# Weight blocks begun one block ahead, and more projection pairs in seven products, in a two-layer encoder trunk

## Chip, cores and metric

The kernel runs on one core of a Trainium2 chip. The metric is the device time of one execution in microseconds (us); three runs of the kernel before took 2011.72, 2015.77 and 2019.56 us, median 2015.77.

## What is computed

Two layers of an encoder over 256 positions of width 2048. Layer 0 mixes positions by dilated window attention, layer 1 by a spatial gate; both run a cross-attention into 256 memory tokens beside the mixer, and both end in a gated FFN with a width-3 convolution. The weight products take nearly all of the time:

```python
for i in range(DEPTH):                       # DEPTH = 2
    h = rmsnorm(x, mix_norm_g[i])
    mem_n = rmsnorm(mem, mem_norm_g[i])
    proj = einsum('bsd,df->bsf', h, a_w_in[j] or b_w_in[j])
    tok = mixer_a(proj[..., :3 * A_QKV_W])   # layer 1: mixer_b(proj[..., :2 * B_W], ...)
    mem_out = memory_cross_attention(proj[..., -MEM_W:], mem_n, w_mem_kv[i])
    x = x + einsum('bsf,fd->bsd', concatenate([tok, mem_out]), w_out)
    h = rmsnorm(x, ffn_norm_g[i])
    x = x + conv_ffn(h, ffn_w_up[i], ffn_conv_w[i], ffn_conv_b[i], ffn_w_down[i])
return rmsnorm(x, final_norm_g)
```

## The kernel before, in words

All weights stream from HBM once, in blocks of 128 x 2048 float32 (1 MB). Products are made at nearly float32 precision from float16 parts: a block is split into `whi` (the rounded value) and `wlo` (the rest), the activations likewise, and a product is hi x hi + hi x lo + lo x hi.

`project_t` (L156 ff.) makes one **pair**: two output tiles of 128 columns for 256 positions, from one or more blocks of up to eight 128-row slices. A pair over the full width of 2048 has two blocks. A block comes in two forms, made by `block_t`:

- *Unformed*: ACT makes `whi` (L138), DVE `wlo` (L139), and TensorE (PE) runs 48 matmuls of 256 columns, 12,288 columns in all.
- *Formed*: the 2 x 2 product of half blocks is made with seven products instead of eight. ACT makes `whi` (L144) and rescales `raw` (L145), DVE makes two halves of `wlo` (L146, L147) and the sums `ws2` and `ws41` (L148, L149; both shown as `ws`), and PE runs 72 matmuls of 256 or 128 columns, 11,264 columns in all. The activations' sums come from `form_sums` (L215 ff.). At the pair's end the parts are put together: ACT copies one part to `wr` (L207), DVE adds (L208, L209, L211, L212), and only then the pair's consumer runs. The last product of a block, into `acc`, reads `ws41`.

In the FFN (`ffn`, L463 ff.) 44 up pairs alternate between gate and value half. Behind each pair ACT runs six taps of the convolution (L481, L482, L483 twice), DVE adds them (L484, L485); behind a gate pair ACT runs the GELU (L487), behind a value pair DVE multiplies (L489) and ACT and DVE split the result into `act` (L246, L247). `UP_FORM` sets which up pairs are formed: the second and fourth of every five, 18 of 44 per FFN. Then eight down pairs follow, seven of them formed in 32 of 44 slices. In the first mixer's input projection every second pair of the loop is formed, in the second mixer's projections none.

A layer's stages follow each other in the program: norm, mixer projections, attention or gate, output projection, norm, up, down. `norm_ready` (L348 ff.) is the norm before an FFN: DVE multiplies (L357) and splits (L247). While it runs, PE works on the memory keys for layer 1 (`kvk`, second pair). In `mixer_b` the value projection `binv` is followed on ACT by two squares (L632), a root with its table load (L261) and the splits of the normalized values (L250), before the pairs of `bin` go on.

The order of the work: a scheduler orders each engine's instructions at build time, by the place in the program and by which buffers are free. There are three `wlo` and `whi` buffers (four `whi` in the FFN), three `raw` buffers (five in the FFN), two of each `ws`, three `acc` and two `accb` banks. Small steps that need not run at once (attention heads, sums) wait in a list, and `step()` runs one of them at the head of each block and in its middle. `fine` counts blocks that are split in four pieces. `keep_clock` runs matmuls without use while PE would idle in a norm.

Of the kernel before, what the change touches and what calls it, by code (L numbers as in the profile page):

```python
# [9 lines left out]
F16 = mybir.dt.float16  # L10
F32 = mybir.dt.float32
# [5 lines left out]
P = 128  # L17
T = 256
# [29 lines left out]

UP_FORM = (False, True, False, True, False)
IN_FORM = (False, True)  # L50
DOWN_K = 32
WARM = (36, 32, 36, 24)


# [5 lines left out]
def trunk(ctx: ExitStack, tc: tile.TileContext, xT, memT, par, w, wsT, sbias, out):  # L60
# [35 lines left out]

    def next_of(name, dtype):
        r = more.get(name, rings[name])
        turns[name] = (turns[name] + 1) % len(r)
        return r[turns[name]].tile([P, KC * FG], dtype, name=name)  # L100

    def block_n(name, g, c, loads=1, beside=None):
        step()
        pieces = FINE if fine[0] > 0 else PIECES
# [16 lines left out]
    def block_t(name, g, k0, kc, form):  # L121

        step()
        pieces = max(1, FINE * kc // KB) if fine[0] > 0 else PIECES
        fine[0] -= 1
        raw = next_of("raw", F32)
        hi = next_of("whi", F16)
        lo = wsp.tile([P, KC * FG], F16, name="wlo")
# [27 lines left out]
    def project_t(name, g, act, nk, evac, sums=None, form=0, before=None, kb=KB):  # L156
        a = acc.tile([P, FG], F32, name="acc")
        b = accb.tile([P, FG], F32, name="accb") if form else None
        done = [0, 0]
        blocks = [(k0, min(kb, nk - k0)) for k0 in range(0, nk, kb)]  # L160
        last = [blocks[-1][0] + blocks[-1][1], min(form, nk)]
# [63 lines left out]
    def project_n(name, g, act, nk, evac, before=None, loads=1, beside=None):  # L225
        ps = [acc.tile([P, FG], F32, name="acc") for _ in range(2)]
        for c in range(nk // KC):
            if before is not None:
                before(c)
            hi, lo = block_n(name, g, c, *((loads, beside) if c == 0 else ()))  # L230
# [208 lines left out]

    def residual(name, act, nk, scale, squares, halves=False, last=False, sums=None, form=0, gain=None):  # L440
        def add_out(g, src):
# [16 lines left out]
        for g in range(KD // 2):  # L458
            project_t(name, g, act, nk, add_out, sums, form if g > 0 else 0)

    xact, xsum = lambda k: xs[:, k, :], lambda k: xu[:, k, :]

    def ffn(i, squares):  # L463
        with tc.tile_pool(name=f"ffw{i}", bufs=1) as fw, tc.tile_pool(name=f"ffr{i}", bufs=2) as fwr, \
# [5 lines left out]
            for g in range(FT):  # L470
# [26 lines left out]
            residual(f"down{i}", lambda k: act[:, k, :], FT, 1.0 / (SW * S_ACT), squares, last=i == 1,  # L497
                     sums=lambda k: room(k, 1)[:, 0, :], form=DOWN_K)
            more.clear()
# [3 lines left out]
    def mixer_a(later):  # L503
        with tc.tile_pool(name="ma", bufs=1) as mp, tc.tile_pool(name="mat", bufs=2) as mt:
# [25 lines left out]

            pending.extend(mem_attention(cat, 0, S_CAT[0]) + [masks] + later)
            sums_later()
            for g in range(3):
                project_n("ainv", g, xs, KD, v_out(g))
# [52 lines left out]
            for g in range(2 * NH * NG // 2):  # L587
                project_t("ain", 2 + g, xact, KD, qk_out, xsum, KD if IN_FORM[g % 2] else 0)
                while done < NH and (done + 1) * 2 * NG <= (g + 1) * 2:
# [11 lines left out]
    def mixer_b():  # L601
        with tc.tile_pool(name="mb", bufs=1) as mp:
            cat = mp.tile([P, BG + NH, 2 * T], F16, name="cat")
            v = mp.tile([P, 2, BG * P], F32, name="v")
            vs = xu.rearrange("p k c -> p (k c)")[:, :4 * BG * P].rearrange("p (t i c) -> p t i c", t=2, i=2)
# [21 lines left out]
            with tc.tile_pool(name="mbt", bufs=2) as mt:  # L627
# [62 lines left out]
    with tc.tile_pool(name="own0", bufs=1) as op:  # L690
        own_tiles(op)
        with tc.tile_pool(name="sums", bufs=1) as sums:
# [27 lines left out]
            for g in range(2):  # L720
                project_t("kv0k", g, mact, KD, k_out, before=lambda c, g=g: x_in(2 * g + c))
            nc.sync.dma_start(out=prm[:, C_CW:], in_=par[:, C_CW:])
            for g in range(2):
                project_t("ain", g, xact, KD, qm_out)
# [102 lines left out]
```

## Time and profile before

| | |
|---|---|
| median of 3 runs | 2015.77 us |
| profiled execution | 2014.48 us |
| its span in the trace | 2012.7 us |
| mean granted clock of TensorE | 0.995 |
| PE busy | 1968.0 us, 98% of the span |
| DVE busy | 1609.1 us, 80% |
| ACT busy | 1418.5 us, 70% |

The span runs from the first to the last instruction of the profiled execution; 1.8 us of its time lie outside. The trace shows for every instruction its start, its length, the idle time of the engine ahead of it and what ended that idle time. The granted clock is the share of 2.4 GHz that TensorE got; it has two levels, 1.2 and 2.4 GHz.

### The profile page before, as it was taken

Reading aid. Unit: us, or ns where it says so; the run is one execution under the profiler, and the core shown is the slowest. Engines: PE = TensorE matmul, PEld = TensorE weight load, DVE = VectorE, ACT = ScalarE, POOL = GpSimd, SP = SyncE. Lnnn points to the kernel's source line nnn. Section 1 sums busy time; section 2 is a strip of 40 time slices with the busy share of each in tenths; the row PEclk is TensorE's granted clock in tenths of the full one; section 3 lists DMA queues with packets and bytes.
Section 4 is the critical chain, followed back from the end, with each engine's and each line's share of the span. In section 5 each row is a group of like instructions: output and inputs, shape, how many; then the busy total and the mean of one; then the engine's idle time right before and its main releaser. Section 6 shows DMA issues by size and latency. Waiting matters only on the chain.

```text
span 2012.7 us, 47883 instructions
## 1 busy us (share of the span) xinstructions
PE 1968.0 (98%) x21200; PEld 1724.7 (86%) x21200; DVE 1609.1 (80%) x1942; ACT 1418.5 (70%) x1649; POOL 2.4 (0%) x9
## 2 busy tenths in 40 slices
PE   8999999999999999999999999999999999999997
PEld 5648888799999999899976489889999999989997
DVE  8867776988888888978877365588888888897885
ACT  7666656887888888666756464577888888866773
POOL 0000000000000000000000000000000000000000
PEclk9999999999999999999999999999999999999999
DMA  8475445656555666466655365546566566645661
GB/s 318 172 259 202 168 151 185 242 206 209 205 210 209 210 210 210 172 216 222 221 210 201 134 212 195 201 179 220 210 210 210 210 210 210 210 168 211 230 221 53
DMA packets 59391, 407.72 MB, mean 203 GB/s; under 512 B 6704, under 2 KB 7344, under 8 KB 12720
## 3 DMA queue, kind: packets, MB, share of 16 engines
q1 hardware_dynamic: 58896, 400.48, 56.2%
q0 software_dynamic: 288, 4.19, 0.5%
q8 instruction: 165, 2.70, 0.5%
q14 instruction: 42, 0.34, 0.0%
HBM read 400.46 MB, written 4.19 MB: 201 GB/s over the span
## 4 chain that ended last, share of the span: by engine, by line
PE 86%; DVE 8%; ACT 3%; DMA 2%; issue 1%; SPq 0%; DVEq 0%; ACTq 0%
PE acc L164 68%; PE accb L164 12%; PE acc L239 2%; PE acc L240 2%; PE acc L238 2%; DVE wlo L139 1%; DVE wlo L118 1%; PE misc L385 1%; ACT whi L138 1%; DMA raw<-w_ainv 1%; DVE xs L247 0%; ACT whi L117 0%; ACT whi L144 0%; DMA raw<-wsT 0%; DVE xu L222 0%
## 5 line engine op out<-in xcount | busy, mean ns | idle before, releaser
L164 PEld LDWEIGHTS <-whi 128*128 128x128 f16 x10880 | 971.2, 98 | 110.5 <-ACT whi L138 6.3
L164 PE MATMUL acc<-xs,whi 128*128 128x256 f16 (+1 forms) x6592 | 797.6, 266 | 9.6 <-ACT whi L138 5.6
L139 DVE SCALAR_TENSOR_TENSOR wlo<-raw,whi 128x2048 f16<-128x2048 f32 (+2 forms) x286 | 465.6, 1644 | 42.9 <-ACT whi L138 40.0
L164 PEld LDWEIGHTS <-wlo 128*128 128x128 f16 x5440 | 443.4, 98 | 50.8 <-DVE wlo L139 10.4
L138 ACT ACTIVATE whi<-raw 128x2048 f16<-128x2048 f32 (+2 forms) x286 | 391.9, 1391 | 131.4 <-PE acc L164 106.4
L144 ACT ACTIVATE whi<-raw 128x2048 f16<-128x2048 f32 x140 | 267.0, 1907 | 117.5 <-PE acc L164 109.5
L164 PE MATMUL acc<-xs,wlo 128*128 128x256 f16 x2176 | 284.0, 273 | 4.8 <-DVE wlo L139 4.8
L164 PE MATMUL acc<-act,whi 128*128 128x256 f16 x2368 | 278.7, 262 | 0.0
L145 ACT ACTIVATE raw<-raw 128x2048 f32<-128x2048 f32 x140 | 267.4, 1910 | 3.0
L146 DVE SCALAR_TENSOR_TENSOR wlo<-whi,raw 128x1024 f16<-128x1024 f16 x140 | 171.1, 1222 | 93.4 <-PE accb L164 48.0
L164 PEld LDWEIGHTS <-ws 128*128 128x128 f16 x3360 | 193.5, 98 | 1.2 <-DVE ws L149 1.0
L149 DVE TENSOR_TENSOR ws<-whi,ws 128x2048 f16<-128x2048 f16 x140 | 170.8, 1220 | 2.7
L147 DVE SCALAR_TENSOR_TENSOR wlo<-whi,raw 128x1024 f16<-128x1024 f16 x140 | 170.6, 1219 | 0.0
L164 PE MATMUL acc<-xu,whi 128*128 128x128 f16 x896 | 154.0, 219 | 0.0
L164 PE MATMUL accb<-xu,ws 128*128 128x128 f16 x1792 | 119.0, 219 | 0.3 <-DVE ws L149 0.2
L484 DVE TENSOR_TENSOR conv<-conv,tap 128x510 f32<-128x510 f32 x88 | 60.6, 689 | 70.6 <-ACT tap L482 69.6
L481 ACT ACTIVATE conv<-wr,prm 128x256 f32<-128x256 f32 x72 | 42.7, 593 | 101.6 <-DVE wr L212 101.6
L118 DVE SCALAR_TENSOR_TENSOR wlo<-raw,whi 128x512 f16<-128x512 f32 (+1 forms) x56 | 75.9, 1373 | 45.5 <-ACT whi L117 38.9
L148 DVE TENSOR_TENSOR ws<-wlo 128x1024 f16<-128x1024 f16 x140 | 96.4, 689 | 2.7
L117 ACT ACTIVATE whi<-raw 128x512 f16<-128x512 f32 (+1 forms) x56 | 63.6, 1170 | 46.4 <-PE acc L164 19.0
L164 PE MATMUL acc<-cat,whi 128*128 128x256 f16 x768 | 91.7, 273 | 0.0
L238 PE MATMUL acc<-whi,xs 128*128 128x512 f16 x192 | 72.8, 379 | 1.6 <-DVE v L251 1.6
(193 smaller groups left out, 1864.7 us busy)
## 6 DMA issues: line engine op xcount, KB each, us to landing
raw<-w_up SPq DMA_DIRECT2D x176, 1024.0 KB, 4.8
raw<-w_down SPq DMA_DIRECT2D x80, 1024.0 KB, 5.0
raw<-w_ain SPq DMA_DIRECT2D x28, 1024.0 KB, 4.8
raw<-w_bin SPq DMA_DIRECT2D x16, 1024.0 KB, 4.9
raw<-w_bout SPq DMA_DIRECT2D x16, 1024.0 KB, 4.8
raw<-w_ainv SPq DMA_DIRECT2D x12, 1024.0 KB, 4.9
raw<-w_binv SPq DMA_DIRECT2D x12, 1024.0 KB, 4.9
raw<-w_aout SPq DMA_DIRECT2D x8, 1024.0 KB, 4.9
```

Of the source, the lines that this page charges most:

```text
L117: S.activation(hi[:, f], raw[:, f], AF.Copy, scale=SW)
L118: V.scalar_tensor_tensor(lo[:, f], raw[:, f], SW, hi[:, f], op0=ALU.mult, op1=ALU.subtract)
L138: S.activation(h, r, AF.Copy, scale=SW)
L139: V.scalar_tensor_tensor(l, r, SW, h, op0=ALU.mult, op1=ALU.subtract)
L144: S.activation(hi[:, :n], raw[:, :n], AF.Copy, scale=SW)
L145: S.activation(raw[:, :n], raw[:, :n], AF.Copy, scale=SW * CX)
L146: V.scalar_tensor_tensor(l[:, 0, :], h[:, 0, :], -CX, r[:, 0, :], op0=ALU.mult, op1=ALU.add)
L147: V.scalar_tensor_tensor(l[:, 1, :], h[:, 1, :], -1.0 - CX, r[:, 1, :], op0=ALU.mult, op1=ALU.add)
L148: V.tensor_tensor(s2[:, :n // 2], l[:, 1, :], l[:, 0, :], op=ALU.subtract)
L149: V.tensor_tensor(s41[:, :n].rearrange("p (j f) -> p j f", j=2), h, s2[:, :n // 2].unsqueeze(1).to_broadcast([P, 2, n // 2]), op=ALU.add)
L164: PE.matmul((a, b)[bank][:, at:at + n], weights, moving, start=done[bank] == 0, stop=stop)
L238: PE.matmul(ps[t], ah, hi[:, k, :], start=(kk == 0), stop=False)
```

## The change

- `AHEAD = 1`: blocks are made by `block()`, which keeps a plan of all blocks in program order. When a block is asked for, the next one in the plan is begun (load and split written into the program) before the asking block's matmuls. Waiting steps run after that.
- `UP_FORM` becomes (False, True): from the fourth up pair on, every second one is formed, 21 of 44 per FFN in place of 18. The first three are unformed.
- Of the eight pairs of the second mixer's output projection `bout`, three (2, 4, 6) are formed; their sums go to a new tile `cu`.
- The second pair of `kvk` becomes an array of its own, `kvl`, with blocks of eight slices in place of four. Empty steps go between the norm's sums. The clock-keeping matmuls read a tile of ones in place of the identity.

```diff
-UP_FORM = (False, True, False, True, False)
+UP_FORM = (False, True)
+AHEAD = 1
...
+    busy = pool.tile([P, P], F16, name="busy")
...
-    def next_of(name, dtype):
-        r = more.get(name, rings[name])
+    def next_of(name, dtype, ffn=False):
+        r = more.get(name, rings[name]) if ffn else rings[name]
...
+    plan, ready = [], {}
+
+    def block(*key):
+        if key in ready:
+            parts = ready.pop(key)
+        else:
+            assert not plan or plan.pop(0) == key
+            parts = (block_t if len(key) == 5 else block_n)(*key)
+        while plan and len(ready) < AHEAD:
+            k = plan.pop(0)
+            ready[k] = (block_t if len(k) == 5 else block_n)(*k)
+        step()
+        return parts
...
-            parts = block_t(name, g, k0, kc, k0 < form)
+            parts = block(name, g, k0, kc, k0 < form)
...
-            PE.matmul(ps[:, :P], ident16, ident16, start=True, stop=True)
+            PE.matmul(ps[:, :P], busy, busy, start=True, stop=True)
...
         for k in range(0, KD, KC):
+            pending.append(lambda: None)
             pending.append(lambda k=k: form_sums(xu[:, k:k + KC, :], xs[:, k:k + KC, :]))
...
-                project_t(f"up{i}", g, xact, KD, conv, xsum, KD if UP_FORM[g % len(UP_FORM)] else 0)
+                project_t(f"up{i}", g, xact, KD, conv, xsum, up_form(g))
...
-                residual("bout", lambda k: cat[:, k, :], BG + NH, 1.0 / (SW * S_CAT[1]), squares, gain=C_FFN + KD)
+                for k in range(0, BG + NH, KC):
+                    pending.append(lambda k=k: form_sums(cu[:, k:k + KC, :], cat[:, k:k + KC, :]))
+                residual("bout", lambda k: cat[:, k, :], BG + NH, 1.0 / (SW * S_CAT[1]), squares, gain=C_FFN + KD,
+                         sums=lambda k: cu[:, k, :], form=bout_form)
...
+    up_form = lambda g: KD if g > 1 and UP_FORM[g % 2] else 0
+    in_form = lambda g: KD if g > 1 and IN_FORM[g % 2] else 0
+    bout_form = lambda g: BG + NH if g in (2, 4, 6) else 0
+    down_form = lambda g: DOWN_K if g > 0 else 0
...
+            planned("up0", range(FT), KD, up_form)
+            planned("down0", range(KD // 2), FT, down_form)
...
-        project_t("kvk", 1, mact, KD, k_out, kb=KC)
+        project_t("kvl", 0, mact, KD, lambda g, src: k_out(1, src))
```

In the changed kernel the lines move: whi and wlo of an unformed block L163, L164; of a formed one L169 to L174 (as L144 to L149); wr L232 to L237 (as L207 to L212); the taps L510 to L512, GELU L516, DVE's additions L513, L514 and product L518, the split of act L274, L275.

ACT in the up projection, from the last tap of one pair to the wr of the next formed pair. In the order before, in every second case, two unformed blocks stand there (and two formed ones in the others):

```order
L483 ACTIVATE tap2_7160<-acc_7161,prm_82 128x256
L138 ACTIVATE whi_7598<-raw_7597 128x2048
L246 ACTIVATE act_4580<-conv0_6969 128x2x256
L138 ACTIVATE whi_7652<-raw_7651 128x2048
L207 ACTIVATE wr_7454<-accb_7285 128x128
L481 ACTIVATE conv0_7281<-wr_7454,prm_82 128x256
```

In the order after, two formed blocks always:

```order
L512 ACTIVATE tap2_7061<-acc_7062,prm_82 128x256
L169 ACTIVATE whi_7430<-raw_7429 128x2048
L170 ACTIVATE raw_7429<-raw_7429 128x2048
L516 ACTIVATE conv0_7059<-conv0_7059 128x512
L169 ACTIVATE whi_7504<-raw_7503 128x2048
L170 ACTIVATE raw_7503<-raw_7503 128x2048
L232 ACTIVATE wr_7353<-accb_7190 128x128
L510 ACTIVATE conv1_7186<-wr_7353,prm_82 128x256
```

The pattern of the steps is now the same in every two pairs; from the first wr of an FFN to the twentieth it repeats 19 times on ACT, and DVE's steps repeat as often.

DVE ahead of the first FFN's norm, from the sum for it to the norm's first product. Before, the `wlo` here are those of the second `kvk` pair, whose third and fourth blocks are 4501 and 4533:

```order
L446 SCALAR_TENSOR_TENSOR x_79<-acc_4329,x_79 128x2x128 x2
L139 SCALAR_TENSOR_TENSOR wlo_4501<-raw_4499,whi_4500 128x2x256 x2
L317 TENSOR_SCALAR mean_4402<-misc_4393 128x2
L262 RECIPROCAL r_tok_4392<-rq_s2_4404 128x2
L263 TENSOR_TENSOR rq_q2_4405<-r_tok_4392 128x2
L264 SCALAR_TENSOR_TENSOR rq_q2_4405<-rq_q2_4405,mean_4402 128x2
L265 SCALAR_TENSOR_TENSOR r_tok_4392<-rq_q2_4405,r_tok_4392 128x2
L323 TENSOR_SCALAR dg_4411<-ident_83,r_tok_4392 128x128
L139 SCALAR_TENSOR_TENSOR wlo_4533<-raw_4531,whi_4532 128x2x256 x2
L357 TENSOR_TENSOR xu_81<-xu_81,misc_4414 128x256 x2
```

After, `wlo_4449` belongs to the last `kvl` block and `wlo_4509` to the first block of the up projection:

```order
L164 SCALAR_TENSOR_TENSOR wlo_4449<-raw_4447,whi_4448 128x2x256 x2
L475 SCALAR_TENSOR_TENSOR x_79<-acc_4341,x_79 128x2x128 x2
L164 SCALAR_TENSOR_TENSOR wlo_4509<-raw_4507,whi_4508 128x2x256 x2
L345 TENSOR_SCALAR mean_4414<-misc_4405 128x2
L164 SCALAR_TENSOR_TENSOR wlo_4509<-raw_4507,whi_4508 128x2x256
L290 RECIPROCAL r_tok_4404<-rq_s2_4416 128x2
L164 SCALAR_TENSOR_TENSOR wlo_4509<-raw_4507,whi_4508 128x2x256
L291 TENSOR_TENSOR rq_q2_4417<-r_tok_4404 128x2
L292 SCALAR_TENSOR_TENSOR rq_q2_4417<-rq_q2_4417,mean_4414 128x2
L293 SCALAR_TENSOR_TENSOR r_tok_4404<-rq_q2_4417,r_tok_4404 128x2
L351 TENSOR_SCALAR dg_4423<-ident_83,r_tok_4404 128x128
L385 TENSOR_TENSOR xu_81<-xu_81,misc_4426 128x256 x2
```

The first up block's `wlo` moved ahead of the norm's products; the second block's stays behind them.

ACT after the second mixer's value projection. Before, the first split of the next `bin` block (15653) stands behind the squares and the root:

```order
L617 ACTIVATE v_14821<-acc_15496 128x512
L632 ACTIVATE raw_15626,ss_15624<-v_14821 128x1536
L617 ACTIVATE v_14821<-acc_15497 128x512
L632 ACTIVATE raw_15626,ss_15624<-v_14821 128x1536
L261 ACT_TABLE_LOAD
L261 ACTIVATE rq_s2_15630<-ss_15624 128x2
L138 ACTIVATE whi_15653<-raw_15652 128x2048
```

After, it is 15816, ahead of them, and the second block (15880) has its old place:

```order
L163 ACTIVATE whi_15816<-raw_15815 128x2048
L648 ACTIVATE v_15048<-acc_15723 128x512
L663 ACTIVATE raw_15853,ss_15851<-v_15048 128x1536
L648 ACTIVATE v_15048<-acc_15724 128x512
L663 ACTIVATE raw_15853,ss_15851<-v_15048 128x1536
L289 ACT_TABLE_LOAD
L289 ACTIVATE rq_s2_15857<-ss_15851 128x2
L163 ACTIVATE whi_15880<-raw_15879 128x2048
```

One block's split moved past five steps.

## Rows read from the trace of the kernel before

**Rows 1.** The page, busy us, share of the span, instructions.

```profile
PE 1968.0 (98%) x21200; PEld 1724.7 (86%) x21200; DVE 1609.1 (80%) x1942; ACT 1418.5 (70%) x1649; POOL 2.4 (0%) x9
```

**Rows 2.** Windows: stretch, length, busy us by engine, granted clock, DMA share, GB/s.

```profile
350.00:400.00 50.00, 45.32 (x441) 39.03 (x439) 48.19 (x72) 39.39 (x49) 0.00 (x0) 0.93 0.66 233
...
409.76:511.63 101.87, 101.87 (x1155) 93.87 (x1153) 86.17 (x91) 83.34 (x104) 0.00 (x0) 1.00 0.60 208
...
800.00:850.00 50.00, 48.26 (x503) 43.72 (x501) 48.57 (x69) 32.41 (x35) 0.00 (x0) 1.00 0.47 169
...
1150.00:1200.00 50.00, 44.39 (x380) 36.26 (x379) 29.82 (x31) 30.28 (x29) 0.00 (x0) 0.93 0.54 190
...
1231.00:1315.00 84.00, 84.00 (x776) 75.33 (x775) 47.87 (x40) 41.34 (x47) 0.00 (x0) 1.00 0.59 203
```

**Rows 3.** Chain of waits: start, us, what; of both FFNs' up and the output projection.

```profile
409.76 24.05 PE acc L164 x232
...
491.40 13.57 PE acc L164 x136
...
511.63 24.05 PE acc L164 x232
...
1219.72 10.48 PE acc L164 x96
```

**Rows 4.** Timeline of ACT, first up projection: start, us, engine, line, [idle before].

```profile
485.41 1.94 ACT L144 ACTIVATE whi<-raw 128x2048 f16<-128x2048 f32 x1
...
493.41 0.26 ACT L207 ACTIVATE wr<-accb 128x128 f32<-128x128 f32 x1
496.67 0.60 ACT L481 ACTIVATE conv<-wr,prm 128x256 f32<-128x256 f32 x1 [3.00 <-DVE wr L212]
...
502.66 0.63 ACT L246 ACTIVATE act<-conv 128x512 f16<-128x512 f32 x1 [1.50 <-DVE conv L489]
...
507.32 1.93 ACT L138 ACTIVATE whi<-raw 128x2048 f16<-128x2048 f32 x1
...
536.34 1.94 ACT L144 ACTIVATE whi<-raw 128x2048 f16<-128x2048 f32 x1
...
557.45 1.93 ACT L138 ACTIVATE whi<-raw 128x2048 f16<-128x2048 f32 x1
...
587.27 1.94 ACT L144 ACTIVATE whi<-raw 128x2048 f16<-128x2048 f32 x1
...
609.19 1.93 ACT L138 ACTIVATE whi<-raw 128x2048 f16<-128x2048 f32 x1
```

**Rows 5.** Waits of ACT, 410 to 800 us: us in total, times, longest.

```profile
ACT act L246 <- DVE conv L489: 15.1, 15, 2.2
ACT whi L138 <- PE acc L164: 9.0, 8, 1.4
```

**Rows 6.** Timeline of DVE beside rows 4.

```profile
495.89 0.69 DVE L212 SCALAR_TENSOR_TENSOR wr<-wr,acc 128x512 f32<-128x512 f32 x1
...
501.94 0.69 DVE L489 TENSOR_TENSOR conv<-conv,conv 128x512 f32<-128x512 f32 x1
502.54 1.22 DVE L149 TENSOR_TENSOR ws<-whi,ws 128x2048 f16<-128x2048 f16 x1
```

**Rows 7.** Timeline of PE where stages meet.

```profile
367.87 0.61 PE L164 MATMUL acc<-xs,wlo 128*128 128x256 f16 x2 [3.97 <-DVE wlo L139]
...
836.88 1.05 PE L164 MATMUL acc<-act,wlo 128*128 128x256 f16 x8 [1.74 <-DVE wlo L139]
...
1162.00 3.60 PE L164 MATMUL acc<-xs,whi 128*128 128x256 f16 x16 [5.61 <-ACT whi L138]
...
1339.11 0.62 PE L164 MATMUL accb<-xs,wlo 128*128 128x128 f16 x8 [0.72 <-DVE wlo L146]
```

**Rows 8.** The page, DMA issues: KB each, us to landing.

```profile
raw<-w_up SPq DMA_DIRECT2D x176, 1024.0 KB, 4.8
```

**Rows 9.** Instructions by line: count | busy us, mean ns | idle before.

```profile
L219 DVE SCALAR_TENSOR_TENSOR xu<-xs 128x512 f16<-128x512 f16 x12 | 8.2, 685 | 0.0
```

More of the change, by code (lines that the diff above doesn't have):

```diff
@@ L95, in trunk, with blocks_of, planned, planned_n @@
     more, turns = {}, {"raw": 0, "whi": 0}
-    def next_of(name, dtype):
-        r = more.get(name, rings[name])
+    def next_of(name, dtype, ffn=False):
+        r = more.get(name, rings[name]) if ffn else rings[name]
         turns[name] = (turns[name] + 1) % len(r)
         return r[turns[name]].tile([P, KC * FG], dtype, name=name)
+    plan, ready = [], {}
[10 more added lines that the diff above has]
+        return parts
+    def blocks_of(nk, kb):
+        return [(k0, min(kb, nk - k0)) for k0 in range(0, nk, kb)]
+    def planned(name, pairs, nk, form=lambda g: 0, kb=KB):
+        plan.extend((name, g, k0, kc, k0 < form(g)) for g in pairs for k0, kc in blocks_of(nk, kb))
+    def planned_n(name, groups):
+        plan.extend((name, g, c) for g in groups for c in range(KD // KC))
     def block_n(name, g, c, loads=1, beside=None):
-        step()
         pieces = FINE if fine[0] > 0 else PIECES
@@ L121, in block_t @@
     def block_t(name, g, k0, kc, form):
-        step()
+        ffn = name[:2] in ("up", "do")
         pieces = max(1, FINE * kc // KB) if fine[0] > 0 else PIECES
         fine[0] -= 1
-        raw = next_of("raw", F32)
-        hi = next_of("whi", F16)
+        raw = next_of("raw", F32, ffn)
+        hi = next_of("whi", F16, ffn)
         lo = wsp.tile([P, KC * FG], F16, name="wlo")
@@ L159, in project_t @@
         done = [0, 0]
-        blocks = [(k0, min(kb, nk - k0)) for k0 in range(0, nk, kb)]
+        blocks = blocks_of(nk, kb)
         last = [blocks[-1][0] + blocks[-1][1], min(form, nk)]
@@ L229, in project_n @@
                 before(c)
-            hi, lo = block_n(name, g, c, *((loads, beside) if c == 0 else ()))
+            if c == 0 and beside is not None:
+                hi, lo = block_n(name, g, c, loads, beside)
+            else:
+                hi, lo = block(name, g, c)
             for t in range(2):
@@ L437, in mem_attention, with residual @@
         return [s[0], s[1], t[0], s[2], v[0], t[1], s[3], v[1], t[2], v[2], t[3], v[3]]
-    def residual(name, act, nk, scale, squares, halves=False, last=False, sums=None, form=0, gain=None):
+    def residual(name, act, nk, scale, squares, halves=False, last=False, sums=None, form=lambda g: 0, gain=None):
         def add_out(g, src):
@@ L458, in residual @@
         for g in range(KD // 2):
-            project_t(name, g, act, nk, add_out, sums, form if g > 0 else 0)
+            project_t(name, g, act, nk, add_out, sums, form(g))
     xact, xsum = lambda k: xs[:, k, :], lambda k: xu[:, k, :]
@@ L497, in ffn @@
             residual(f"down{i}", lambda k: act[:, k, :], FT, 1.0 / (SW * S_ACT), squares, last=i == 1,
-                     sums=lambda k: room(k, 1)[:, 0, :], form=DOWN_K)
+                     sums=lambda k: room(k, 1)[:, 0, :], form=down_form)
             more.clear()
@@ L532, in mixer_a @@
             sums_later()
+            assert len(pending) <= 24
             for g in range(3):
@@ L587, in mixer_a @@
             for g in range(2 * NH * NG // 2):
[L588 removed]
+                project_t("ain", 2 + g, xact, KD, qk_out, xsum, in_form(2 + g))
                 while done < NH and (done + 1) * 2 * NG <= (g + 1) * 2:
@@ L603, in mixer_b @@
             cat = mp.tile([P, BG + NH, 2 * T], F16, name="cat")
+            cu = mp.tile([P, BG + NH, 2 * T], F16, name="cu")
             v = mp.tile([P, 2, BG * P], F32, name="v")
@@ L722, in trunk @@
             nc.sync.dma_start(out=prm[:, C_CW:], in_=par[:, C_CW:])
+            planned("ain", range(2), KD)
+            planned_n("ainv", range(3))
+            planned("ain", range(2, 2 + NH * NG), KD, in_form)
+            planned("kvk", range(1), KD, kb=KC)
+            planned("aout", range(KD // 2), 2 * NH)
+            planned("kvl", range(1), KD)
+            planned("up0", range(FT), KD, up_form)
+            planned("down0", range(KD // 2), FT, down_form)
+            planned_n("kvv", range(1))
+            planned("bin", range(2), KD)
+            planned_n("binv", range(3))
+            planned("bin", range(2, 8), KD)
+            planned("bout", range(KD // 2), BG + NH, bout_form)
+            planned("up1", range(FT), KD, up_form)
+            planned("down1", range(KD // 2), FT, down_form)
             for g in range(2):
@@ L800 @@
     arrays["w_kv0v"] = blocks(kv[0][:, FG:])
-    arrays["w_kvk"] = pairs(kv[1][:, :FG], KC)
+    arrays["w_kvk"] = pairs(kv[1][:, :PW], KC)
+    arrays["w_kvl"] = pairs(kv[1][:, PW:FG])
     arrays["w_kvv"] = blocks(kv[1][:, FG:])
```

1 line of the change is left out of this document (added).

## The prediction

> **What bounds the kernel now.** I read the page's busy shares first [rows 1]. PE is at 98%, DVE at 80% and ACT at 70%, so by shares alone PE is the bound. A mean over stages with different limits cannot carry a prediction, so next come the windows [rows 2]. From 409.76 to 511.63 us, ten pairs of the first up projection, PE is busy for all of 101.87 us, DVE for 86.17 and ACT for 83.34. PE idles mainly where stages meet.
>
> The chain of waits gives PE's prices [rows 3]. An unformed pair is 96 matmuls in 10.48 us. The ten pairs hold six unformed and four formed ones, so a formed pair costs (101.87 - 6 x 10.48) / 4 = 9.75 us: it saves PE 0.73. An unformed and a formed pair together take PE 20.23 us.
>
> The third view is the one that matters most, ACT's timeline in the same stretch [rows 4]. From 485.41 ACT goes through: first half of a formed pair's split, GELU, second half, the copy into wr (493.41), the six taps of that formed pair (from 496.67), an unformed block's split, the split of act (502.66), another unformed split, the six taps of an unformed pair, and at 507.32 the next weight split. That is ACT's whole work for one unformed and one formed pair, and it took 21.91 us; the next time it came, 587.27 to 609.19, 21.92. PE needs 20.23 for the same two pairs. ACT lost two waits in it, 3.0 us from wr to the taps and 1.5 before act, both for DVE and neither for PE. Before the change this does no harm, because two of five pairs are formed: after each U F U F comes a second U, which gives ACT room to catch up. How little room is left, the list of waits shows [rows 5]: from 410 to 800 us ACT waited only 9.0 us for PE's buffers.
>
> **The change, part by part.** Here U is an unformed pair, F a formed one.
>
> 1. *Half the up pairs.* F goes from 18 to 21 of 44 in each FFN. For PE that is 3 x 0.73 = 2.2 us less in each: 448.0 us becomes 445.8 (23 x 10.48 + 21 x 9.75). But from the fourth pair on the pattern is now U F U F without the second U, and the order shows ACT's steps repeating in just the sequence of rows 4, 19 times in each FFN, with DVE's steps in the same order too. The two waits repeat with it, since their causes do: DVE can start its sums only when ACT has copied wr, and works on a ws step (1.2 us) between them, so that wr is finished at 495.89 + 0.69 and the taps start 3.26 us after the copy; DVE's product for act (501.94) stands behind the taps and two weight steps [rows 6]. Nothing in this circle asks PE for anything, so a slower PE would not shorten it.
>
>    I take 21.92 us for the circle. The last matmuls of a formed pair end at 491.85 (491.40 and 8 matmuls of 0.056, [rows 3]), and ACT copies wr 1.6 us later. So the up stage is: U U U F = 41.2 us; 1.6 to the first copy; 19 x 21.92 = 416.5; then from the 20th copy to the end of the last F, whose second ws is done at 502.54 + 1.22, 10.35 after a copy [rows 6], and 16 matmuls of 0.056 behind it, 11.3 in all. Sum 470.6 against 448.0 without stalls: **+22.6 in each FFN, +45.2**. The buffers' lead is in that sum: it hides the first four circles. Bounds: 21.11 us, which the same nine steps took where GELU and act change places (536.34 to 557.45, [rows 4]), gives +14.4 for both FFNs; 22.6, with the longest act wait of rows 5 (2.2), gives +71. I stay with 21.92, since its sequence is the same instruction by instruction.
>
>    Occupancy says otherwise. ACT's busy time in the circle is 21.92 - 4.5 = 17.4 us, 86% of PE's 20.23. The Trainium skill, "Perfetto Trace Analysis", section Identifying the Most-Contended Engine, calls occupancy a fair measure of how close Vector and Scalar engines are to their limit; by it PE would stay the bound at 445.8. Rows 4 speak against that: ACT is occupied for 82% of rows 2's stretch and still left hardly any time unexplained by DVE.
>
> 2. *A block ahead, at the first up projection.* PE waited 3.97 us at 367.87 for wlo of the first block, which DVE did behind the norm [rows 7]; the clock then fell, and the slice 350 to 400 shows 0.93 [rows 2], that is up to 0.07 x 50 = 3.5 us. The order now has that block's wlo before the norm's first step, the second block's still behind it. I take a stall of 3 in place of 7.4: **-4.4** (between 0, if the second block inherits the wait, and -7.4).
>
> 3. *The second up projection* began with a formed pair second, which waited 0.72 us for its wlo at 1339.11, the first of four such waits [rows 7]; U U U now comes first: **-2** (0 to -3).
>
> 4. *After the second mixer's value projection* PE waited 5.61 us at 1162.00 for whi, behind two squares, a table load and a root on ACT [rows 7], and the clock shows 0.93 again. That block's split now stands ahead of them; PE has 5.24 us of matmuls (half of 10.48) while the next split runs where this one did. Left is about 0.5 of waiting, twice, and no fall: **-5.5** (0 to -8).
>
> 5. *Three formed pairs of the output projection*: 3 x 0.73 = **-2.2**. Their sums (DVE, 16 instructions of 0.69 us at most, 11 us [rows 9]) and longer splits lie beside PE: from 1231 to 1315 us DVE is busy 47.87 of 84 and ACT 41.34 [rows 2]. Without that cover the sums alone would cost their 11 us.
>
> 6. *At nothing:* the 1 MB loads, each a place earlier in SP's queue, land in 4.8 us [rows 8] against some 10 us of PE work for two; the clock-keeping matmuls keep their number; the memset and the dummy steps lie in idle places. The starts of both down projections (1.74 us at 836.88) I leave as they are, give or take 2.
>
> Sum: 45.2 - 4.4 - 2 - 5.5 - 2.2 = **+31.1** on the profiled execution's 2014.48 us, **2046**. The median of the runs, 2015.77, is 1.3 above it; I don't shift for that. With the bounds of the small terms and a circle of 21.7 to 22.2 us this case spans 2030 to 2060.
>
> **The rivals.** *PE stays the bound (faster).* If the two waits shrink by 1.7 us together once ACT is behind, the up stages take 445.8 each: -4.4 instead of +45.2, so -18.5, **1996**. For it: 82% occupancy, a PE that never stands still in 101.87 us of rows 2, and splits that sit a pair ahead. Against it: neither wait of rows 4 names PE. It decides at a circle of 20.23.
>
> *Half-way (no change).* A circle of 21.11 gives 41.2 + 1.6 + 19 x 21.11 + 11.3 = 455.2 for a stage, +14.4 for both, and -14.1 from the rest: **2015**. For it: the same steps have run in that time; against it: in another order.
>
> *The clock falls as well (slower yet).* PE would now stand still some 1.7 us in about 15 circles of each FFN. In rows 2 and 7 a wait of 1.74 left the clock at 1.00 (800 to 850), while waits of 3.97 and 5.61 were followed by 0.93. If the short ones, repeated, bring it down, each costs PE up to 3.5 us; a PE circle of 23.7 exceeds ACT's, stalls end and the clock returns, so about half: 38 x 1.8 / 2 = +34, **2080**. The Trainium skill, "TensorE: Matmul & The Clock Gate", section A second HAM failure mode, tells of micro-idles between matmul groups making the clock swing between its two levels; by that rule this case would be the likely one. The one short wait in rows 7 does not agree.
>
> That the block ahead changes little is part of the forecast: the scheduler already ran splits early, and only items 2 to 4 move.
>
> **How the numbers follow.** Forecast 0.71, PE bound 0.17, half-way 0.08, clock 0.04. The predicted time is the forecast's, 2046. The range, 2010 to 2068, holds the forecast with most of the bounds of its circle, the half-way case and the start of the clock case, and leaves out the faster one. Faster by over 0.5% (what a measurement here can tell from no change, 10 us): 0.17. Within 0.5%: the half-way case and the forecast's far edge, 0.10. Slower: 0.73.
>
> **What would show it.** Right: in both up stages the chain repeats every 21.9 us, PE waits some 1.7 us for ws (L174) about 15 times in each, ACT's wait for wr is about 3.0 in each circle and for act 1.5, and ACT's waits for PE vanish there; the PE waits for wlo after the first norm and for whi at the second mixer are under 2 us. Wrong: a period of 20.2 with ACT waiting for PE (then the first rival), or a granted clock under 1.00 inside the up stages (then the third). If the up stages behave and the total misses, items 2 to 4 were mis-sized.

## The result: 2050 us, 1.8% slower, as forecast

The changed kernel takes 2050.43 us (median of 4 runs, 2050.12 to 2052.02) beside 2015.05 for the kernel before in the same comparison: a ratio of 1.0176, 95% interval 1.0155 to 1.0197. The forecast was 2046, with a range of 2010 to 2068. The profiled execution took 2050.40 us, its span is 2048.6.

The page's first part after the change (busy us, share of the span, instructions) answers to [rows 1]:

```profile
PE 1976.4 (96%) x21632; PEld 1721.9 (84%) x21632; DVE 1654.9 (81%) x2066; ACT 1458.1 (71%) x1693; POOL 2.4 (0%) x9
```

PE fell from 98% to 96%; DVE and ACT each rose by one point. The shares hardly tell what happened. The chain of waits does (start, us, what), here in the first up projection, with only the pieces that repeat:

```profile
536.25 1.91 ACT raw L170
...
540.54 0.70 DVE wr L237
...
546.67 0.61 DVE conv L518
...
558.20 1.91 ACT raw L170
...
562.49 0.70 DVE wr L237
...
568.62 0.61 DVE conv L518
...
580.14 1.91 ACT raw L170
```

Before, this chain consisted of PE alone, in pieces of 24.05 and 13.57 us [rows 3]. Now PE is on it only up to 482 us. From there to the end of the stage it runs over ACT and DVE and comes back after 21.95 us (558.20 - 536.25, 580.14 - 558.20). ACT's timeline shows the same circle, with the two waits of [rows 4] (start, us, engine, line, [idle before]):

```profile
560.01 0.26 ACT L232 ACTIVATE wr<-accb 128x128 f32<-128x128 f32 x1
563.27 0.60 ACT L510 ACTIVATE conv<-wr,prm 128x256 f32<-128x256 f32 x1 [3.00 <-DVE wr L237]
...
569.25 0.63 ACT L274 ACTIVATE act<-conv 128x512 f16<-128x512 f32 x1 [1.50 <-DVE conv L518]
...
581.96 0.26 ACT L232 ACTIVATE wr<-accb 128x128 f32<-128x128 f32 x1
```

ACT's waits from 410 to 800 us (total, times, longest) are these two and no other. The 9.0 us for PE's buffers of [rows 5] are gone, since PE is no longer late for ACT:

```profile
ACT conv L510 <- DVE wr L237: 54.0, 18, 3.0
ACT act L274 <- DVE conv L518: 26.9, 18, 1.5
```

PE pays for it. From the circle on in which its lead over ACT is used up, it stands still once in each, for ws (L174), 16 times in the first up projection and 17 in the second. PE's timeline has the first two of these stops, the last one with the first matmul of the down projection behind it, the first stop of that projection, and the place of the 5.61 us of [rows 7], where 0.37 is left:

```profile
504.57 0.62 PE L189 MATMUL accb<-xu,ws 128*128 128x128 f16 x8 [1.02 <-DVE ws L174]
...
526.52 0.62 PE L189 MATMUL accb<-xu,ws 128*128 128x128 f16 x8 [1.12 <-DVE ws L174]
...
833.79 0.62 PE L189 MATMUL accb<-xu,ws 128*128 128x128 f16 x8 [1.12 <-DVE ws L174]
834.24 0.61 PE L189 MATMUL acc<-xs,ws 128*128 128x128 f16 x8
834.69 1.91 PE L189 MATMUL acc<-act,whi 128*128 128x256 f16 x16
...
855.05 1.05 PE L189 MATMUL acc<-act,wlo 128*128 128x256 f16 x8 [2.56 <-DVE wlo L164]
...
1180.23 1.92 PE L189 MATMUL acc<-xs,whi 128*128 128x256 f16 x16 [0.37 <-ACT whi L163]
```

The windows (length, busy us of PE, PEld, DVE, ACT, POOL, granted clock, DMA share, GB/s) show that the clock had no part in the loss. It is 1.00 in both up stages, and 1.00 in the two slices that had 0.93 in [rows 2]:

```profile
350.00:400.00 50.00, 49.52 (x479) 43.57 (x477) 47.53 (x76) 39.88 (x60) 0.00 (x0) 1.00 0.61 220
365.80:836.00 470.20, 450.64 (x5202) 408.20 (x5200) 392.05 (x451) 375.66 (x460) 0.00 (x0) 1.00 0.57 197
...
1150.00:1200.00 50.00, 49.35 (x351) 32.90 (x349) 29.07 (x28) 31.01 (x30) 0.00 (x0) 1.00 0.54 190
1337.00:1810.00 473.00, 453.12 (x5226) 410.82 (x5225) 395.51 (x457) 375.16 (x462) 0.00 (x0) 1.00 0.56 194
```

Where the time went, by stage, from the first matmul of one to the first of the next in PE's timeline (us, rounded):

| Stage | before | after | change | forecast |
|---|---|---|---|---|
| up to the first up projection | 362.0 | 361.0 | -1.0 | 0 |
| first up projection | 455.5 | 473.7 | +18.2 | +18.2 |
| first down projection, through its second pair's formed part | 49.8 | 52.6 | +2.8 | 0 |
| rest of the first down projection | 174.2 | 174.1 | -0.1 | 0 |
| second mixer, to its output projection | 189.2 | 181.1 | -8.1 | -5.5 |
| its output projection | 92.2 | 89.0 | -3.2 | -2.2 |
| second up projection | 452.4 | 476.9 | +24.5 | +20.6 |
| second down projection, same part | 49.8 | 52.6 | +2.8 | 0 |
| rest | 187.7 | 187.6 | -0.1 | 0 |
| sum | 2012.7 | 2048.6 | +35.9 | +31.1 |

### The profile page after: what moved, and what is told of

Its sections match the earlier page's. It is cut to its first block, busy times and chain, and to the rows that moved or that the text cites. A ratio compares the mean times of both kernels' runs of the same rounds, so it can differ in the third digit from the quotient of the medians.

```text
span 2048.6 us, 48916 instructions
## 1 busy us (share of the span) xinstructions
PE 1976.4 (96%) x21632; PEld 1721.9 (84%) x21632; DVE 1654.9 (81%) x2066; ACT 1458.1 (71%) x1693; POOL 2.4 (0%) x9
## 4 chain that ended last, share of the span: by engine, by line
PE 49%; ACT 27%; DVE 17%; issue 6%; DMA 1%; SPq 0%; DVEq 0%; ACTq 0%; POOLq 0%
PE acc L189 34%; PE accb L189 7%; ACT whi L169 6%; ACT raw L170 6%; ACT whi L163 4%; ACT tap L511 3%; ACT conv L510 3%; DVE ws L174 2%; PE acc L267 2%; PE acc L268 2%; PE acc L266 2%; ACT tap L512 2%; DVE wlo L164 2%; DVE conv L513 1%; DVE conv L514 1%
## 5 line engine op out<-in xcount | busy, mean ns | idle before, releaser
L189 PEld LDWEIGHTS <-wlo 128*128 128x128 f16 x5440 | 429.5, 98 | 52.6 <-DVE wlo L164 18.0
L164 DVE SCALAR_TENSOR_TENSOR wlo<-raw,whi 128x512 f16<-128x512 f32 (+2 forms) x285 | 425.8, 1511 | 23.0 <-ACT whi L163 22.8
L163 ACT ACTIVATE whi<-raw 128x512 f16<-128x512 f32 (+2 forms) x285 | 357.8, 1283 | 88.4 <-PE acc L189 59.6
L169 ACT ACTIVATE whi<-raw 128x2048 f16<-128x2048 f32 x158 | 301.9, 1911 | 109.4 <-PE acc L189 102.6
L170 ACT ACTIVATE raw<-raw 128x2048 f32<-128x2048 f32 x158 | 302.0, 1911 | 4.6
L171 DVE SCALAR_TENSOR_TENSOR wlo<-whi,raw 128x1024 f16<-128x1024 f16 x158 | 192.9, 1221 | 101.3 <-ACT raw L170 52.9
L189 PEld LDWEIGHTS <-ws 128*128 128x128 f16 x3792 | 217.2, 98 | 50.1 <-DVE ws L174 41.8
L189 PE MATMUL acc<-xs,wlo 128*128 128x256 f16 x1984 | 258.6, 273 | 0.4 <-DVE wlo L164 0.2
L174 DVE TENSOR_TENSOR ws<-whi,ws 128x2048 f16<-128x2048 f16 x158 | 192.3, 1217 | 1.9
L172 DVE SCALAR_TENSOR_TENSOR wlo<-whi,raw 128x1024 f16<-128x1024 f16 x158 | 192.3, 1217 | 0.0
L189 PE MATMUL accb<-xu,ws 128*128 128x128 f16 x1984 | 137.2, 219 | 39.1 <-DVE ws L174 36.1
L510 ACT ACTIVATE conv<-wr,prm 128x256 f32<-128x256 f32 x84 | 49.8, 593 | 130.7 <-DVE wr L237 130.7
L513 DVE TENSOR_TENSOR conv<-conv,tap 128x510 f32<-128x510 f32 x88 | 60.6, 689 | 72.5 <-ACT tap L511 72.5
L189 PE MATMUL accb<-xs,wlo 128*128 128x128 f16 x992 | 75.6, 219 | 0.0
```

The source lines that it names most:

```text
L163: S.activation(h, r, AF.Copy, scale=SW)
L164: V.scalar_tensor_tensor(l, r, SW, h, op0=ALU.mult, op1=ALU.subtract)
L169: S.activation(hi[:, :n], raw[:, :n], AF.Copy, scale=SW)
L170: S.activation(raw[:, :n], raw[:, :n], AF.Copy, scale=SW * CX)
L171: V.scalar_tensor_tensor(l[:, 0, :], h[:, 0, :], -CX, r[:, 0, :], op0=ALU.mult, op1=ALU.add)
L172: V.scalar_tensor_tensor(l[:, 1, :], h[:, 1, :], -1.0 - CX, r[:, 1, :], op0=ALU.mult, op1=ALU.add)
```

## The experiments

The theory to be tested: ACT's instructions in their order, with two waits for DVE, make a circle of 21.95 us and set both up stages; PE, with 20.23, does not. The rivals: PE's own matmuls, DVE's load, or the block ahead.

### The old pattern back

```diff
-UP_FORM = (False, True)
+UP_FORM = (False, True, False, True, False)
...
-    up_form = lambda g: KD if g > 1 and UP_FORM[g % 2] else 0
+    up_form = lambda g: KD if g > 1 and UP_FORM[g % 5] else 0
```

> The changed kernel with the old pattern of up pairs (U F U F U, the first two pairs unformed: 17 formed in each FFN); the block ahead, the three formed pairs of the output projection and all else stay. Theory (the ACT circle of one U and one F pair, 21.95 us against PE's 20.23, costs the time): the second U of each five gives ACT its room back, no waits of PE for ws recur, both up stages fall back to 452 to 456 us from 473.7 and 477.0, and the time is 2050.4 - 19 - 23 = 2008 us (2002 to 2013), under the kernel before by the gains of the other parts. Rival (the block ahead, or what else was moved, slows the up stages): the time stays above 2035 and waits for ws or for whi recur in the up stages.

Measured: 1993.33 us, ratio to the kernel before 0.9891 (0.9873 to 0.9909). No wait for ws recurs, and the up stages take 449.6 and 451.6 us. The theory holds, and its expectation was 15 us too high: the up stages fell by 24.1 and 25.3 us where 19 and 23 were expected, and the starts of the two down projections came down with them, from 52.6 to 47.9 us each, so these belong to the pattern as well. The pattern costs 57 us here, and the rest of the change, on its own, gains 24.

### The wr copy on DVE

```diff
-        S.activation(r[:, :P], b[:, :P], AF.Copy)
+        V.tensor_copy(r[:, :P], b[:, :P])
```

> The changed kernel with one instruction of each formed pair moved: the copy of accb's first quarter into wr is done by DVE ahead of its own sums, and no longer by ACT. Theory (the circle is ACT's instructions in order plus its two waits for DVE): the copy and most of the 3.0 us wait behind it leave ACT's order, ACT is free to go on, the circle falls under about 20.7 us and PE becomes the bound or nearly so: up stages of 447 to 455 us, 2000 us in all (1993 to 2010), with ACT waiting for PE again. Rival 1 (DVE's work is what fills the circle): DVE has some 0.3 us more in each of 38 circles, so the time rises to about 2060. Rival 2 (the two waits on ACT are only the image of a late PE): no change, 2048 to 2053.

Measured: 1989.97 us, 0.9873 (0.9856 to 0.9891). One instruction of 0.26 us, moved, takes 60 us off the changed kernel, more than the expectation's 1993 to 2010 allowed. ACT's timeline shows a circle of 20.41 us (590.69 - 570.28) in which one of the two waits is 1.62 instead of 3.00:

```profile
570.28 0.60 ACT L510 ACTIVATE conv<-wr,prm 128x256 f32<-128x256 f32 x1 [1.62 <-DVE wr L237]
...
576.26 0.63 ACT L274 ACTIVATE act<-conv 128x512 f16<-128x512 f32 x1 [1.50 <-DVE conv L518]
...
590.69 0.60 ACT L510 ACTIVATE conv<-wr,prm 128x256 f32<-128x256 f32 x1 [1.62 <-DVE wr L237]
```

That is 0.18 above PE's 20.23, so in 19 circles ACT falls back by 3.4 us. PE doesn't wait once between 410 and 800 us, so the buffers' lead covers that, and the up stages take 446.7 and 448.7 us, near PE's own 445.8. In the first FFN the chain of waits is PE's again up to 658 us; from there it follows ACT and DVE, and their lag ends in the first stops of the down projection (1.02 and 0.34 us), not in the up stage:

```profile
563.04 13.57 PE acc L189 x136
576.61 1.79 PE accb L189 x32
578.39 3.09 PE acc L189 x40
581.48 1.79 PE accb L189 x32
583.27 13.57 PE acc L189 x136
...
657.51 0.91 PE accb L189 x16
...
658.45 1.89 ACT whi L163
```

That ACT would wait for PE again, as expected, did not come true. DVE has more to do than before the move (1657.5 us beside 1654.9), so a bound by DVE's load falls, and so does the idea that the two waits are the image of a late PE.

### Idle matmuls, 18 and then 14

```diff
+        if name[:2] == "up":
+            keep_clock(18)
```

> The changed kernel with 18 matmuls of 128x128 more (0.056 us each, 1.0 us, into a bank that nobody reads) at the end of each of the 42 formed up pairs: 42 us of work for PE. Theory (PE has 1.7 us to spare in each circle that ACT sets): PE's waits for ws shrink by about 1.0 us in each circle, the circle stays 21.95 us, and the time grows by what is not covered in the first circles of each up stage alone, 0 to 5 us: 2050 to 2056. Rival (PE's matmuls bound the up stages): 42 us more, about 2092.

Measured: 2066.66 us, 1.0251 (1.0230 to 1.0272). That is 16 us more than the changed kernel, neither theory's number. The scheduler had set DVE's splits and ACT's GELU in other places, and ACT's second wait grew from 1.50 to 2.02 us:

```profile
609.74 0.60 ACT L512 ACTIVATE conv<-wr,prm 128x256 f32<-128x256 f32 x1 [3.00 <-DVE wr L239]
...
616.25 0.63 ACT L276 ACTIVATE act<-conv 128x512 f16<-128x512 f32 x1 [2.02 <-DVE conv L520]
```

The wr copies are 22.34 us apart in this run, 0.39 more than 21.95. Over 35 circles (the second FFN's first three are still 21.95) that is 13.7 of the 16 us. So the run spoke for ACT's order, but its edit had not left the two engines' order alone. The next one did, but for two split pieces on ACT that change places once in each FFN:

```diff
+        if name[:2] == "up":
+            keep_clock(14)
```

> As the run with 18 idle matmuls, with 14 in their place (0.78 us, 33 us of PE's work in the 42 formed pairs): with 18 the order of DVE's and ACT's steps in the circle had changed too, with 14 it is that of the changed kernel. Theory (ACT's order and its two waits for DVE set the circle): wr copies 21.95 us apart as before, PE's wait for ws of 1.28 us shrinks to about 0.5, and the time grows by 0 to 3 us: 2050 to 2054. Rival (PE bounds): 33 us more, 2083.

Measured: 2050.30 us (1.0170, 1.0155 to 1.0185); the changed kernel has 2050.43. So 33 us of additional PE work cost nothing. ACT's timeline has the wr copy every 21.96 us, and PE's has its stops for ws cut from 1.12 to 0.77 us (part of the room that PE had lay in smaller pauses between its matmuls):

```profile
537.58 0.26 ACT L234 ACTIVATE wr<-accb 128x128 f32<-128x128 f32 x1
...
559.54 0.26 ACT L234 ACTIVATE wr<-accb 128x128 f32<-128x128 f32 x1
...
581.50 0.26 ACT L234 ACTIVATE wr<-accb 128x128 f32<-128x128 f32 x1
```

```profile
591.90 0.62 PE L189 MATMUL accb<-xu,ws 128*128 128x128 f16 x8 [0.77 <-DVE ws L174]
```

PE is not the bound there, as plainly as it can be shown.

### The block ahead taken away, with either pattern

```diff
-AHEAD = 1
+AHEAD = 0
```

> The changed kernel with no block begun ahead (AHEAD = 0), the pattern U F and the three formed pairs of the output projection kept. Theory (the circle is set by ACT's order in the steady stage, which one block ahead does not alter): the circle stays 21.9 us in both up stages; what is lost are the gains at the first up projection (4.4 as predicted, the wait for wlo at its start is back) and behind the second mixer's value projection (5.5, the wait for whi of 5 to 6 us is back), so 2060 us (2056 to 2064). Rival (the block ahead itself lengthens the circle, since the splits of the next pair now stand in front of the taps): the circle falls to 21.1 us or less and the time to 2045 or less.

Measured: 2064.78 us, 1.0243 (1.0226 to 1.0261), 0.8 above the expected range, and the wr copies 21.96 us apart: the block ahead has no part in the circle. The same edit with the old pattern:

> The changed kernel with the old pattern (as in the first run) and no block begun ahead. It tells what the block ahead is worth where ACT does not set the up stages: against the 1993 us of the old pattern with the block ahead. Theory: 6 to 7 us more behind the second mixer's value projection (the wait for whi is back), 2 us at the start of each down projection, 2 us at the first up projection: 2006 us (2002 to 2010). Rival (the whole gain at the first up projection is the block ahead's, as the prediction had it): its stage is 5 to 6 us longer and the time 2010 us or more. A second rival (the block ahead is worth nothing outside these places): under 2000.

Measured: 2005.61 us, 0.9942 (0.9925 to 0.9959), where the theory had 2006. The four medians make a square:

| | block ahead | none | what it gives |
|---|---|---|---|
| old pattern | 1993.3 | 2005.6 | -12.3 |
| U F pattern | 2050.4 | 2064.8 | -14.4 |
| what the pattern costs | +57.1 | +59.2 | |

The two parts hardly touch each other. Without the block ahead, the wait at the second mixer is back; with the U F pattern PE's timeline has:

```profile
1185.48 1.89 PE L189 MATMUL acc<-xs,whi 128*128 128x256 f16 x8 [5.61 <-ACT whi L163]
```

From the mixer's first projection of its normed input to a block behind its value projection it takes 110.0 us instead of 103.2. Another gain lies where none was forecast: with the U F pattern the starts of the down projections take 55.8 and 56.2 us without it, 52.6 with it (48.6 and 47.9 with the old one). The first up projection itself hardly changes (473.9 and 473.7 us with the U F pattern, 451.0 and 449.6 with the old one). But without the block ahead PE waits for whi right ahead of that stage's first matmul, which the stage table counts to the stage before. With the old pattern:

```profile
362.50 1.13 PE L189 MATMUL acc<-xs,whi 128*128 128x256 f16 x8 [1.49 <-ACT whi L163]
```

Counted to the first matmul of the down projection, the block ahead gives 3.4 us with the old pattern (813.46 and 810.09) and 0.8 with U F (835.51 and 834.69), where ACT's circle sets the end of the stage.

### The pattern alone, in the kernel before

```diff
-UP_FORM = (False, True, False, True, False)
+UP_FORM = (False, True)
...
-                project_t(f"up{i}", g, xact, KD, conv, xsum, KD if UP_FORM[g % len(UP_FORM)] else 0)
+                project_t(f"up{i}", g, xact, KD, conv, xsum, KD if g > 1 and UP_FORM[g % 2] else 0)
```

> The kernel before with the pattern of the up pairs alone changed (U F from the third pair on, 21 formed in each FFN); no block ahead, no formed pairs in the output projection. Theory (ACT's circle, set by the pattern alone): the wr copies of both up stages are 21.95 us apart; up stages of 474 and 477 us from 455.5 and 452.3, and the starts of both down projections longer by 5 to 6 us each, since ACT and DVE arrive late there: 2015 + 18.5 + 24.7 + 11 = 2069 us (2060 to 2075). Rival (part of the circle comes from the blocks begun ahead): copies 21.1 us apart or less and a time of 2045 or less.

Measured: 2082.12 us, 1.0320 (1.0303 to 1.0337), and the same circle: 21.95 or 21.96 between wr copies, 19 times in each FFN. It is 13 us above the expectation. The first copy came later in the first FFN (50.1 us after the stage's first matmul, where the changed kernel needs 45.4), and the down projections' starts grew by 7.2 and 8.8 us. There PE stands still three times (its timeline):

```profile
852.19 1.05 PE L164 MATMUL acc<-act,wlo 128*128 128x256 f16 x8 [2.07 <-DVE wlo L139]
...
860.41 1.56 PE L164 MATMUL acc<-act,wlo 128*128 128x256 f16 x8 [2.80 <-DVE wlo L139]
...
869.37 1.05 PE L164 MATMUL acc<-act,wlo 128*128 128x256 f16 x8 [1.88 <-DVE wlo L139]
```

### A block's split ahead of the side work

The kernels without the block ahead had lost the 3.97 us wait for wlo of [rows 7] too (two waits for whi, 1.49 and 0.43 us, stand in its place), so something else in the change took part in it. One candidate is the place of step(), which the change moves behind a block's own split. In the kernel before, with that alone (the same in block_n):

```diff
     def block_t(name, g, k0, kc, form):
-        step()
...
             parts = block_t(name, g, k0, kc, k0 < form)
+            step()
```

> The kernel before with one thing moved: a block's own split is written ahead of the waiting side work of that place (the sums of the mixer's or the first up projection's input among it), not behind it; nothing is begun a block ahead. The run with the old pattern and no block ahead had lost the wait of 3.97 us for wlo at the first up projection all the same. Theory (that wait came from the four sums that DVE did ahead of the first block's wlo, and the place of the side work took it away, not the block ahead): the wait for wlo falls under 1 us, the clock stays at 1.00 there, the first up stage is 3 to 5 us shorter than 455.5, the wait of 5.6 us for whi at the second mixer stays: 2012 us beside 2016 (2009 to 2014). Rival (the wait moves to the second block or stays): 2015 to 2018.

Measured: 2011.16 us, 0.9973 (0.9962 to 0.9983). The time is where it was expected, the mechanism only in part: PE's wait for wlo is 2.70 us, not under 1, and the first up stage took 455.2 us beside 455.5, where 3 to 5 us less were expected. What the shorter wait gave came back in two stops for ws that the kernel before doesn't have:

```profile
366.76 0.39 PE L162 MATMUL acc<-xs,wlo 128*128 128x256 f16 x2 [2.70 <-DVE wlo L137]
...
384.82 0.62 PE L162 MATMUL accb<-xu,ws 128*128 128x128 f16 x8 [0.79 <-DVE ws L147]
...
392.10 0.62 PE L162 MATMUL accb<-xu,ws 128*128 128x128 f16 x8 [0.59 <-DVE ws L147]
```

DVE's timeline accounts for the 2.70. It starts that wlo at 366.01, right behind the split of the memory keys (km) that follows the norm; in the kernel before three steps of the sums (1.27 us) stood between, and 3.97 - 1.27 = 2.70:

```profile
365.41 0.69 DVE L251 SCALAR_TENSOR_TENSOR km<-ja,km 128x512 f16<-128x512 f32 x1
366.01 2.49 DVE L137 SCALAR_TENSOR_TENSOR wlo<-raw,whi 128x512 f16<-128x512 f32 x4
```

The same two steps in the run with the old pattern and no block ahead come 1.85 us earlier:

```profile
363.56 0.68 DVE L279 SCALAR_TENSOR_TENSOR km<-ja,km 128x512 f16<-128x512 f32 x1
364.16 2.49 DVE L164 SCALAR_TENSOR_TENSOR wlo<-raw,whi 128x512 f16<-128x512 f32 x4
```

What made them earlier was not tried by itself. Of the 1.85 us, 1.36 are there already at the norm's first step on DVE, which waits for PE (mean, 352.57 and 351.21), so most of it comes from the order of PE's work ahead of the norm. The memory's second pair of keys, which PE works on there and which now has an array of its own and blocks of another size, is the nearest candidate. Also left open is where the 5 us of the medians lie, of which the two profiled spans show only 1.0; the profiled execution here, 2013.42 us, is 2.3 above its median.

### The output projection without formed pairs

```diff
-                for k in range(0, BG + NH, KC):
-                    pending.append(lambda k=k: form_sums(cu[:, k:k + KC, :], cat[:, k:k + KC, :]))
...
-    bout_form = lambda g: BG + NH if g in (2, 4, 6) else 0
+    bout_form = lambda g: 0
```

> The changed kernel with no formed pair in the second mixer's output projection and without the sums of its input (16 steps of DVE); all else stays. Theory (PE bounds that projection, each formed pair saves it 0.73 us and the start is unchanged): the stage is 2 to 3.5 us longer, the time 2053 us (2051 to 2055). Rival (the stage got shorter by its start, not by the formed pairs): no change in the stage, 2050.

Measured: 2051.12 us, 1.0173 (1.0158 to 1.0188), which can't be told from the changed kernel's 2050.43. The stage itself takes 91.2 us instead of 89.0: 2.2 for three pairs, 0.73 each. The third microsecond that the stage had lost against the kernel before is not the pairs': the run with the pattern alone, without formed pairs there, has 91.2 us as well.

### Towards a better kernel

The copy on DVE, with the last pair of each up projection left unformed:

```diff
-        S.activation(r[:, :P], b[:, :P], AF.Copy)
+        V.tensor_copy(r[:, :P], b[:, :P])
...
-    up_form = lambda g: KD if g > 1 and UP_FORM[g % 2] else 0
+    up_form = lambda g: KD if 1 < g < 43 and UP_FORM[g % 2] else 0
```

> The kernel with the wr copy on DVE (1990 us), and the last pair of each up projection unformed: 20 formed in place of 21. Theory (ACT and DVE arrive late at the down projections, whose starts waited 1.2 and 2.9 us for wlo): PE works 0.73 us longer in each up stage, the waits at the starts go: 1988 us (1985 to 1990). Rival (those waits come from the order at the start itself): 1991 us, with both waits still there.

Measured: 1988.05 us, 0.9862 (0.9844 to 0.9880), the fastest of all, if hardly to be told from 1989.97. The starts of the down projections take 47.9 and 48.5 us, where the copy on DVE alone had 49.6 and 51.3. And the copy on DVE with the old pattern:

> The kernel with the old pattern (1993 us) and the wr copy on DVE as well. Theory (the copy on DVE helps where ACT sets the time alone; with the old pattern PE does): no change, 1991 to 1995, up stages within 1 us of 449.6 and 451.6. Rival (the copy on DVE is worth something in every formed pair, wherever it is): 1985 us or less.

Measured: 1993.79 us, 0.9888 (0.9866 to 0.9909): nothing gained (1993.33 with the copy on ACT), and up stages of 449.6 and 451.6 us. The copy on DVE pays only where ACT sets the time. With it, the U F pattern is worth 4 to 6 us instead of costing 57.

## Why the prediction was right, and where its sizes were not

**The circle (step 1)** was right in its mechanism and its period: 21.92 forecast, 21.95 measured, 19 times in each FFN, with waits of 3.00 and 1.49 us (54.0 / 18 and 26.9 / 18). From the 20th copy to the end of the stage it took 11.3 us (823.38 to 834.69), as worked out. PE's stops for ws were 1.12 us where some 1.7 was forecast, because 0.6 of its room lay in smaller pauses (21.95 - 1.12 = 20.83, beside 20.23). The term that was mis-sized is the circle's beginning, "U U U F = 41.2 us; 1.6 to the first copy", 42.8 in all. The first copies came 45.4 and 48.6 us after the stages' first matmuls (406.37 - 360.98 in the first): ACT, too, had been held up where the stages meet, by the norm and the first blocks' splits in small pieces. In the first FFN the 3 us of stalls that step 2 had left made up for that; the stage is 473.7 beside a forecast of 473.6, which is luck. In the second, 2.4 us were left (452.4 - 448.0 - 2) and the copy came 5.8 late, so **3.9 us** of the total's error lie there.

The stalls that ACT's lag causes and those at a stage's start don't add: PE's lead is used up either way, and the stage ends 19 circles and 11.3 us after ACT's first copy.

**Occupancy.** ACT was busy for 375.66 of 470.20 us, 80%, in the stage whose time it set, and PE for 96%. The Trainium skill's measure, "Perfetto Trace Analysis", Identifying the Most-Contended Engine, would have named PE, by its weight loads too (408.20 us, 87%); the run with 14 idle matmuls shows that PE had room. ACT, whose order of steps is fixed when the kernel is built, was full with 17.45 us of work and 4.50 of waits for DVE in 21.95.

**First up projection (step 2).** The wait went, and more than -4.4 with it, but only in part by the block ahead. With the old pattern, where PE sets the stage, the down projection starts 7.4 us earlier than in the kernel before (810.09 and 817.51) with one formed pair fewer; 3.4 of them are the block ahead's. The rest goes with an earlier DVE and the other parts; the place of step() took 1.27 us off the wait but by itself hardly shortened the stage (455.2 beside 455.5). In the changed kernel ACT's circle hides most of this.

**Second up projection (step 3).** The four waits at its start (0.72 and 0.41 us for wlo, 0.13 and 0.17 for ws) are gone. With the old pattern the stage is 0.8 us shorter with one formed pair fewer (0.73), so the -2 was about right; in the changed kernel ACT's circle hides it.

**The mixer (step 4)** was mis-sized by 2.6 us (-8.1 for -5.5). The block ahead gave 6.9 of it by the runs without it. PE's wait fell from 5.61 to 0.37 us, and with the clock at 1.00 instead of 0.93 PE was busy in the stage for 179.94 us instead of 181.85; the forecast's 5.5 leaves 0.9 for the clock, beside a wait shortened by 4.6.

**Output projection (step 5)**: 2.2 forecast, 2.2 by the experiment, 3.2 in the comparison of the stages; the last 1.0 goes with the pattern.

**"At nothing" (step 6)** was wrong at one place: the starts of the down projections, 2.8 us longer each where "give or take 2" was allowed for. Two effects met there: ACT and DVE arrive late from the circle (4.7 us more than with the old pattern), and the other parts of the change make up some of it (with the old pattern these starts are 1.9 us shorter than in the kernel before).

**Rivals.** PE as the bound (1996) came true only when one copy was moved. The half-way case did not appear: no circle was shorter than 21.94. The third rival, a falling clock, is refuted by the windows: 33 stops for ws, and 1.00 in both up stages. The rule in the Trainium skill, "TensorE: Matmul & The Clock Gate", A second HAM failure mode, by which micro-idles between matmul groups make the clock swing, does not show in these stages.

All told, the prediction lay 4 us low. The pattern cost 57 us and the rest gave back 24 (the square, and its distance to the kernel before), where 45.2 and 14.1 were forecast: they were too small by 12 and 10, and the errors covered each other. That the total came so close is luck in this part; the circle, which is most of it, is not.

## What to carry to other kernels

Before an order of work is made denser, write down for each engine one whole circle of its steps, its waits for other engines included, and compare its length with the busiest engine's; an engine at 80% can be the one that sets the time. Where it does, look for the small instruction that makes it wait twice (here a 0.26 us copy that handed work to DVE and then waited 3 us for its return) and give it to the engine that uses its result. And when an experiment adds work for one engine, see whether the other engines' order is still the same before its time is read.

## What the runs showed beyond that

Fourteen idle matmuls per formed pair, 33 us of TensorE work in all, changed the time by less than can be measured; eighteen cost 16 us, of which 13.7 lie in ACT's longer circle. And the granted clock did not follow the sum of PE's idle time: 33 pauses of about 1.1 us left it at 1.00, while in the profile with the pattern alone three pauses of 1.88 to 2.80 us stood in a slice at 0.97:

```profile
850.00:900.00 50.00, 43.25 (x486) 38.76 (x485) 45.78 (x56) 30.14 (x23) 0.00 (x0) 0.97 0.63 222
```

Nor does the length of one pause decide it. In the changed kernel a stop of 2.56 us for wlo stands at the start of each down projection (855.05 and 1828.81); the slice with the first shows 1.00, the one with the second 0.97:

```profile
850.00:900.00 50.00, 45.95 (x551) 42.01 (x550) 48.55 (x60) 38.42 (x27) 0.00 (x0) 1.00 0.59 211
1815.00:1865.00 50.00, 47.44 (x529) 42.70 (x527) 49.76 (x65) 34.89 (x30) 0.00 (x0) 0.97 0.61 221
```
